# Three paces of one encoder step: transposed decode weights, held stores and one left operand

## The chip, the cores and the metric

The kernel runs on one core of one Trainium2 chip. The metric is the device time of one execution in microseconds (us). Engines: TensorE (PE; its weight loads are PEld), VectorE (DVE), ScalarE (ACT), GpSimd (POOL) and SyncE (SP). Each takes the instructions of its own queue in the order in which the program left them there; transfers are issued from such a queue too.

## The reference, cut to what matters

One layer of a streaming encoder with two kinds of heads, 8 each of width 128. The prompt is one stream of 1024 frames of width 2048; the samples are 8 running streams of 16 frames, with 1024 cached frames each.

```python
h = rms_norm(x, norm_pre)
q_sb, k_sb, v_sb, gate_sb, q_r, k_r, v_r, gate_r = split(h @ w_in)   # q_r, k_r with rope
# stick-breaking attention, strictly causal
z = q_sb @ k_sb.T * HEAD_DIM ** -0.5
log_keep = where(strict, log_sigmoid(-z), 0)
later = cumsum(log_keep, reverse=True) - log_keep
o_sb = where(strict, exp(log_sigmoid(z) + later), 0) @ v_sb
# retention, chunks of 64, state carried on
o_r = (q_r @ k_r.T * intra) @ v_r + (q_r @ s) * decay_read
s = s * gamma ** n + (k_r * decay_write).T @ v_r
# merge
y = concat(head_norm(o_sb) * g_sb * silu(gate_sb), head_norm(o_r) * g_r * silu(gate_r))
x = x + rms_norm(y @ w_out, norm_post)
```

For the samples the same with k_all = concat(cache, k) and v_all = concat(cache, v). Besides x, the new keys, values and states are returned.

## The kernel before, in words

**Products.** Each product of float32 matrices is made of three matmuls of rounded halves: high by high, high by low, low by high. A split is two instructions: ScalarE copies the source into the high half (L174), VectorE subtracts that from the source into the low half (L175). Weights land in `wr` or `wrn` and become `wh` and `wl`, or `whn` and `wln`. Left operands of the last stage land in `mr` and become `mh` and `ml`. Such three matmuls are called a turn.

**Stages.** The tokens are in two groups: group 0 has prompt tiles 0 to 3 and the samples, group 1 prompt tiles 4 to 7. Group 0's heads run from about 30 to 1040 us of the span, group 1's from 1040 to 1860, and then the output projection to the end. In a head the projections run on TensorE all the time (L416 and L473), and attention and retention are laid between them. The output projection is seven products of half-size blocks in the manner of Strassen (numbers 5, 1, 3, 2, 6, 7, 4), each for group 0 and group 1, on lines 1306, 1309 and 1310.

**Paces.** Work beside the projections is written as Python generators. Each time a turn has been recorded, one step of the jobs is recorded too, and `yield n` means "go on n turns later". The numbers of turns are the table at the head of the file. From what was recorded a scheduler then builds each engine's queue; stores and loads with `pin` keep their place in their queue. So a pace shifts where an instruction is recorded, and the queues show where it ends.

**Decode, L862 on.** For each head the 128 rows of the samples against 1024 cached and 128 new keys: scores, sigmoids, a scan on VectorE. The weights go through DRAM to be turned (out on L698, in on L709), VectorE transposes blocks of 32 in place (L942, `kp`), then comes `yield D_TD`, one matmul with the new values (L945, `pd`), and two sets of sixteen with the cached values (L953), each after its own wait `D_VC`, then the evacuation on L961 and L963.

**Out.finish, L769 on.** The outputs of a head are normalised and gated (L771), turned through DRAM in the same manner (`s_o`, L698 and L709), transposed on VectorE (L782), multiplied by the gain (L783), and stored to `s_y` from ScalarE's queue (L786), for group 1 with waits `D_HELD` and pinned. `so` is the tile for stick-breaking, `ro` the one for retention.

**The last stage's operands.** `both(n, groups)`, L1463, makes the jobs that load and split the left operands of product n: `left` loads pairs of `mr` on SyncE (L344, three buffers deep), waits `D_LEFT // 2` = 12 turns, and then splits them one after another. The weights `wr` of the projection are loaded on SyncE (L1323, five buffers). The table `then` starts product 2's operand for group 0 beside product 1 of group 0, whose `left(0, 2)` is read from `s_y`.

Of the kernel before, what the change touches and what calls it, by code (L numbers as in the profile page):

```python
# [47 lines left out]
D_HELD = 7  # L48
# [7 lines left out]
V_SET = 4  # L56
D_SUM = 6
EARLY = 6
D_TD = 7
D_OFF = 3  # L60
N_READ = 40
D_FIN = 2
# [2 lines left out]
D_LEFT = 24  # L65
D_SUM2 = (4, 6, 26)
D_SUM3 = (3, 3, 6)
MR = 3
# [26 lines left out]
def tile_hybrid_step(  # L95
# [48 lines left out]
    wp = ctx.enter_context(tc.tile_pool(name="wp", bufs=4))  # L144
# [27 lines left out]
    def split(hi, lo, src):  # L172
        return (
            nc.scalar.activation(hi, src, AF.Copy),  # L174
            nc.vector.tensor_tensor(lo, src, hi.bitcast(F32), ALU.subtract),  # L175
        )

    def split_pre(hi, lo, src, k):
        return (
            nc.scalar.activation(hi, src, AF.Copy, scale=pre[:, k : k + 1]),  # L180
            nc.vector.scalar_tensor_tensor(  # L181
                lo, src, pre[:, k : k + 1], hi.bitcast(F32), ALU.mult, ALU.subtract
            ),
        )
# [14 lines left out]
    def pin(*made):  # L199
        if anchor[0] is not None:  # L200
            for ins in made:
                tc.add_manual_dep(
                    ins.ins,
                    anchor[0].ins.name,
                    mybir.DependencyInfo(mybir.DependencyClass.NoSync, mybir.DependencyReason.SCHED_ONLY),
                    reason="not ahead of the products",
                )
# [126 lines left out]
    def left(gi, n, hi, lo, bufs, tag, deep, wait, spare=None):  # L334
        src = LEFT[n]
        raw = []

        def load(pair, r=None):
            r = bufs.tile([P, 2, 256], F32, name=tag, tag=tag, bufs=deep) if r is None else r
            if src[0] == "y":  # L340
                rows = s_y[gi][src[1] * H // 2 + pair][:, :, src[2] * 256 : src[2] * 256 + 256]
            else:
                rows = s_s[gi][pair][:, :, src[1], :]
            pin(nc.sync.dma_start(r, rows))  # L344
            raw.extend((r[:, 0], r[:, 1]))

        for pair in range(deep):
            load(pair)
        yield wait
        ahead = deep  # L350
        if spare is not None:
            load(deep, spare.pop().rearrange("p t j d -> p (t j d)")[:, :512].rearrange("p (i n) -> p i n", i=2))
            ahead += 1
            yield 0
        for h in range(HT):
            pin(*split(hi[h], lo[h], raw.pop(0)))
            if h % 2 and h // 2 + deep >= ahead and h // 2 + deep < HT // 2:
                load(h // 2 + deep)
            yield D_OP
# [127 lines left out]
    with ExitStack() as s1:  # L487
# [46 lines left out]
        with tc.tile_pool(name="p0", bufs=2) as p0, tc.tile_pool(name="p0s", bufs=1) as p0s, tc.tile_pool(  # L534
# [97 lines left out]
            for piece, (o, m) in enumerate(X_PIECES[:2]):  # L632
                for w in range(KT // WQ):
# [3 lines left out]
                    for j in range(WQ):  # L637
                        k = w * WQ + j
                        hi, lo = (half[w][:, j, o : o + m] for half in mov)
                        made = split_pre(hi, lo, xc[:, j, :], k)  # L640
# [117 lines left out]
        class Out:  # L758
# [9 lines left out]
            def finish(self, b, gi, h, at, oT, dst):  # L768
                rs = inv_rms(op, self.ssq, P, "o")  # L769
                for i in range(self.nt):  # L770
                    nc.vector.scalar_tensor_tensor(  # L771
                        self.o[:, i, :], self.o[:, i, :], rs[:, i : i + 1], gated[gi, h][:, at + i, b, :], ALU.mult, ALU.mult
                    )
                if gi == 1:
                    yield D_HELD
                s = turn_out(self.o, f"s_o{b}_{h}_{self.nt}_{gi}", held=gi == 1)
                yield D_TO[phase[0]] - (D_HELD if gi == 1 else 0)
                flat = self.o.rearrange("p k d -> p (k d)")
                turn_in(s, flat, back[phase[0]])
                yield D_TI[phase[0]]  # L780
                n = self.nt * P
                tied(nc.vector.transpose(oT[:, :n], flat))  # L782
                nc.vector.tensor_scalar(flat, oT[:, :n], gains[:, b, h : h + 1], None, ALU.mult)  # L783
                if gi == 1:
                    yield D_HELD
                store = nc.scalar.dma_start(dst, flat)  # L786
                if gi == 1:
                    pin(store)
# [76 lines left out]
        def decode(h, qs, rest):  # L865
# [76 lines left out]
            tied(nc.vector.transpose(kp[:, :n], be))  # L942
            yield D_TD
            po = psd.tile([P, 512], F32, name="pd", tag="pd")
# [198 lines left out]
        summed, sampled, lefts, mine = [], [], [], {}  # L1143
        held_over, spare = [], []

        def kept(i):
            return [[half[i][:, h // 2, h % 2 * 256 : h % 2 * 256 + 256] for h in range(HT)] for half in mov]
# [18 lines left out]
        for gi, g in enumerate(GROUPS):  # L1166
            tiles, n, nt = g["tiles"], g["n"], len(g["tiles"])
# [161 lines left out]
        made = collections.deque()  # L1329
# [64 lines left out]
    with ExitStack() as s3:  # L1394
        c3 = s3.enter_context(tc.tile_pool(name="c3", bufs=1))
        rp = s3.enter_context(tc.tile_pool(name="rp", bufs=1))
# [66 lines left out]
        def both(n, groups):  # L1463
            made = []
            for g in groups:
                mine[g, n] = operand(c3, ("ah", "al"), 256, bufs=2) if g else kept(at[n])
                made.append(left(g, n, *mine[g, n], *((rp, "yr", 2) if g else (wp, "mr", MR)), D_LEFT // 2))
            return made

        def jobs_of(made):  # L1470
# [34 lines left out]
        more = Job(sums(fp, [sum_rows(1, h) for h in range(EARLY, H)], D_SUM3, 3), 30)  # L1505
# [202 lines left out]
```

## Time and profile before

| what | us |
|---|---|
| median of three runs (2231.7, 2233.36, 2233.37) | 2233.36 |
| the profiled execution's own time | 2233.32 |
| its span | 2231.6 |
| TensorE busy in the span | 2216.6 (99%) |
| VectorE, ScalarE, GpSimd busy | 1263.4, 920.8, 424.5 |
| 34775 instructions, 12046 of them matmuls | |

The span goes from the first to the last instruction; 1.7 us of the time lie around it. A matmul of 512 columns is listed with 0.39 us, and the next starts 0.23 us after it, since matmuls overlap. In the views a row of waits gives total us, number and longest; a row of the timeline gives start, duration, engine, line, what is written and read, and in brackets the idle time before it with what ended it.

### The profile page before, as it was taken

The numbers are of one execution on the slowest core, as the hardware profiler recorded it, in microseconds if no ns is written. First come the engines' busy times: TensorE is split into PE (matmuls) and PEld (weight loads), VectorE is DVE, ScalarE is ACT, GpSimd is POOL, SyncE is SP. The second block draws the span as 40 slices with busy tenths as digits, with TensorE's granted clock in tenths as the row PEclk, the third lists the DMA queues.
The fourth block names the chain that finished last, engine by engine and source line by source line (L and its number), as shares of the span: only waits on it lengthen the run. The fifth ranks groups of instructions, "written<-read, shape, count | busy, mean of one in ns | idle before, by whom it ended". The sixth has DMA issues, their size and how long they took to land. (4 is left out here: it accounts for less than half of the span.)

```text
span 2231.6 us, 34775 instructions
## 1 busy us (share of the span) xinstructions
PE 2216.6 (99%) x12046; PEld 1887.5 (85%) x12046; DVE 1263.4 (57%) x2690; ACT 920.8 (41%) x1999; POOL 424.5 (19%) x715
## 2 busy tenths in 40 slices
PE   9999999999999999999999999999999999999998
PEld 8888889798888979888788888888888888878887
DVE  5435445453544545346566666757665757656677
ACT  6424333333333333334444343443434445545563
POOL 1022131222213122221222111120202212000020
PEclk9999999999999999999999999999999999999999
DMA  8567565576656557668768787878778777865785
GB/s 295 174 199 199 178 185 181 177 193 217 178 184 184 182 176 195 217 179 289 226 197 230 229 231 221 237 229 237 229 228 223 222 233 197 241 215 166 219 224 170
DMA packets 387234, 467.83 MB, mean 210 GB/s; under 512 B 126321, under 2 KB 243825, under 8 KB 386545
## 3 DMA queue, kind: packets, MB, share of 16 engines
q1 hardware_dynamic: 258928, 291.63, 44.2%
q0 software_dynamic: 36048, 94.67, 15.6%
q10 hardware_dynamic: 92080, 79.32, 11.3%
q8 instruction: 94, 1.54, 0.3%
q14 instruction: 84, 0.68, 0.1%
HBM read 364.56 MB, written 106.95 MB: 211 GB/s over the span
## 5 line engine op out<-in xcount | busy, mean ns | idle before, releaser
L473 PE MATMUL accm<-whn,ml 128*128 128x512 f32 x1152 | 452.3, 393 | 0.0
L473 PE MATMUL accm<-whn,mh 128*128 128x512 f32 x1152 | 451.6, 393 | 0.5 <-DVE rq L519 0.5
L473 PE MATMUL accm<-wln,mh 128*128 128x512 f32 x1152 | 451.9, 392 | 0.0
L174 ACT ACTIVATE wh<-wr 128x512 fp32r<-128x512 f32 x408 | 256.7, 631 | 466.2 <-PE acc L416 191.2
L416 PE MATMUL acc<-ml,wh 128*128 128x256 f32 (+2 forms) x1536 | 446.3, 341 | 0.7 <-DVE ml L181 0.3
L416 PE MATMUL acc<-mh,wl 128*128 128x256 f32 (+2 forms) x1536 | 443.9, 340 | 0.0
L416 PE MATMUL acc<-mh,wh 128*128 128x256 f32 (+2 forms) x1536 | 441.4, 338 | 0.2
L175 DVE TENSOR_TENSOR wl<-wr,wh 128x512 fp32r<-128x512 f32 x408 | 279.4, 688 | 264.6 <-ACT wh L174 244.7
L175 DVE TENSOR_TENSOR wln<-wrn,whn 128x512 fp32r<-128x512 f32 x256 | 175.5, 688 | 285.2 <-ACT whn L174 281.5
L174 ACT ACTIVATE whn<-wrn 128x512 fp32r<-128x512 f32 x256 | 161.2, 631 | 384.4 <-PE accm L473 261.4
L416 PEld LDWEIGHTS acc<-mh,wl 128*128 128x128 f32 x1536 | 281.3, 188 | 23.8 <-issue 5.4
L416 PEld LDWEIGHTS acc<-mh,wh 128*128 128x128 f32 x1536 | 283.0, 188 | 21.0 <-ACT mh L180 0.9
L416 PEld LDWEIGHTS acc<-ml,wh 128*128 128x128 f32 x1536 | 280.3, 188 | 21.1 <-DVE ml L181 1.6
L473 PEld LDWEIGHTS accm<-whn,mh 128*128 128x128 f32 x1152 | 216.5, 188 | 44.6 <-DVE rq L519 0.9
L473 PEld LDWEIGHTS accm<-whn,ml 128*128 128x128 f32 x1152 | 216.5, 188 | 43.2 <-issue 0.8
L473 PEld LDWEIGHTS accm<-wln,mh 128*128 128x128 f32 x1152 | 216.5, 188 | 43.2 <-DVE wln L175 0.3
L745 DVE TENSOR_TENSOR_SCAN kp<-kp 128x1152 f32<-128x1152 f32 (+4 forms) x40 | 82.6, 2064 | 55.9 <-POOL kp L734 28.1
L709 POOL DMA_DIRECT2D be<-s_be x120 | 87.8, 738 | 128.2 <-DMA s_be<-be 128.2
L1306 PE MATMUL a<-wh,mh 128*128 128x512 f32 x240 | 94.7, 395 | 0.1
L1309 PE MATMUL a<-wl,mh 128*128 128x512 f32 x240 | 93.8, 391 | 0.3 <-DVE wl L175 0.2
L1310 PE MATMUL a<-wh,ml 128*128 128x512 f32 x240 | 93.6, 390 | 0.0
L734 POOL TENSOR_SCALAR_AFFINE_SELECT kp<-kp 128x128 f32<-128x128 f32 x40 | 13.8, 345 | 369.2 <-ACT kp L728 369.2
(289 smaller groups left out, 3013.2 us busy)
## 6 DMA issues: line engine op xcount, KB each, us to landing
wrn<-w_rows SPq DMA_DIRECT2D x256, 256.0 KB, 3.9
wr<-w_cols SPq DMA_DIRECT2D x255, 256.0 KB, 4.4
kcT<-cache_k POOLq DMA_DIRECT2D x64, 512.0 KB, 4.7
vc<-cache_v SPq DMA_DIRECT2D x64, 512.0 KB, 5.3
wr<-s_b SPq DMA_DIRECT2D x80, 256.0 KB, 3.4
wr<-w_out SPq DMA_DIRECT2D x80, 256.0 KB, 4.3
br<-w_out SPq DMA_DIRECT2D x64, 256.0 KB, 4.6
s_b<-br ACTq DMA_DIRECT2D x32, 512.0 KB, 4.5
```

Of the source, the lines that this page charges most:

```text
L174: nc.scalar.activation(hi, src, AF.Copy),
L175: nc.vector.tensor_tensor(lo, src, hi.bitcast(F32), ALU.subtract),
L416: last = nc.tensor.matmul(a[:, :m], lhs[:, j, :], rhs[w][:, j, o : o + m], start=(w == 0 and j == 0 and n == 0), stop=(w == KT // WQ - 1 a ...
L473: anchor[0] = nc.tensor.matmul(banks[t], lhs[q][:, j, ts], rhs, start=(k == 0 and n == 0), stop=(k == KT - 1 and n == 2),)
L709: (last if last and i == 3 else q).dma_start(raw[32 * i : 32 * i + 32, :].rearrange("p (k a) -> p k a", a=32), s[:, :, 32 * i : 32 * i + 3 ...
L734: nc.gpsimd.affine_select(blk, blk, pattern=[[-1, P]], base=0, channel_multiplier=1, compare_op=ALU.is_gt, fill=fill,)
L745: nc.vector.tensor_tensor_scan(rev, rev, rev, 1.0, ALU.mult, ALU.bypass)
L1306: ins = nc.tensor.matmul(a, hi[k][:, ts], wh, start=first, stop=False)
L1309: nc.tensor.matmul(a, hi[k][:, ts], wl, start=False, stop=False)
L1310: anchor[0] = nc.tensor.matmul(a, lo[k][:, ts], wh, start=False, stop=last)
```

## The change

Three numbers. `D_TD`, the wait between the transpose of the decode weights and the first matmul that reads them, goes from 7 turns to 9. In `Out.finish` the wait before group 1's store goes from 7 turns to 14. In `both` the wait before the splits of the left operand of product 2 for group 0 goes from 12 turns to 16. A line is added in `both`, so lines from 1465 on have one more.

```diff
-D_TD = 7
+D_TD = 9
...
                 nc.vector.tensor_scalar(flat, oT[:, :n], gains[:, b, h : h + 1], None, ALU.mult)
                 if gi == 1:
-                    yield D_HELD
+                    yield 2 * D_HELD
                 store = nc.scalar.dma_start(dst, flat)
...
                 mine[g, n] = operand(c3, ("ah", "al"), 256, bufs=2) if g else kept(at[n])
-                made.append(left(g, n, *mine[g, n], *((rp, "yr", 2) if g else (wp, "mr", MR)), D_LEFT // 2))
+                more = 4 if (g, n) == (0, 2) else 0
+                made.append(left(g, n, *mine[g, n], *((rp, "yr", 2) if g else (wp, "mr", MR)), D_LEFT // 2 + more))
```

No instruction is added or taken away. In group 0 the queues of SyncE, ScalarE and GpSimd stay as they are. On TensorE, in decode head 0, the first set and L945 keep their place, and the second set of L953 moves. Its rows before, with the turns around it (`acc` is the projection's sum, `pd` the decode output, the numbers name buffers):

```order
L416 MATMUL acc0_2125<-ml3_158,wh_2275 128x256
L416 MATMUL acc1_2126<-ml3_158,wh_2275 128x384
L953 MATMUL pd_2144<-vc_1999,kp_1197 32x256 x4
L953 MATMUL pd_2144<-vc_2053,kp_1197 32x256 x4
L953 MATMUL pd_2144<-vc_2181,kp_1197 32x256 x4
L953 MATMUL pd_2144<-vc_2183,kp_1197 32x256 x4
L416 MATMUL acc0_2125<-mh3_157,wl_2276 128x256
L416 MATMUL acc1_2126<-mh3_157,wl_2276 128x384
L416 MATMUL acc0_2336<-mh0_151,wh_2340 128x256
L416 MATMUL acc1_2337<-mh0_151,wh_2340 128x384
```

and now:

```order
L416 MATMUL acc0_2125<-mh3_157,wl_2276 128x256
L416 MATMUL acc1_2126<-mh3_157,wl_2276 128x384
L416 MATMUL acc0_2320<-mh0_151,wh_2324 128x256
L416 MATMUL acc1_2321<-mh0_151,wh_2324 128x384
L416 MATMUL acc0_2320<-ml0_152,wh_2324 128x256
L416 MATMUL acc1_2321<-ml0_152,wh_2324 128x384
L953 MATMUL pd_2148<-vc_1999,kp_1197 32x256 x4
L953 MATMUL pd_2148<-vc_2053,kp_1197 32x256 x4
L953 MATMUL pd_2148<-vc_2201,kp_1197 32x256 x4
L953 MATMUL pd_2148<-vc_2203,kp_1197 32x256 x4
L416 MATMUL acc0_2320<-mh0_151,wl_2325 128x256
```

The set moved behind six matmuls of the projection; heads 1 to 5 show the same, and head 6 a move by two matmuls.

In group 1 neighbours change places at many points. One is the end of head 6, at about 1750 us. On VectorE, before (`be` and `so` on L782 and L783 are the turned outputs, L745 and L746 the attention scan of the next rows):

```order
L745 SCALAR_TENSOR_TENSOR kp_17388<-kp_17388 128x640
L782 STREAM_TRANSPOSE be_16850<-so_16433 128x512
L746 TENSOR_TENSOR be_17389<-be_17389,kp_17388 128x640
L783 TENSOR_SCALAR so_16433<-be_16850,pre_77 128x512
L175 TENSOR_TENSOR wln_17510<-wrn_17507,whn_17509 128x512
L175 TENSOR_TENSOR wln_17559<-wrn_17556,whn_17558 128x512
L175 TENSOR_TENSOR wln_17595<-wrn_17592,whn_17594 128x512
```

and now:

```order
L782 STREAM_TRANSPOSE be_16853<-so_16434 128x512
L783 TENSOR_SCALAR so_16434<-be_16853,pre_77 128x512
L745 SCALAR_TENSOR_TENSOR kp_17389<-kp_17389 128x640
L746 TENSOR_TENSOR be_17390<-be_17390,kp_17389 128x640
L175 TENSOR_TENSOR wln_17513<-wrn_17510,whn_17512 128x512
L175 TENSOR_TENSOR wln_17548<-wrn_17545,whn_17547 128x512
L175 TENSOR_TENSOR wln_17595<-wrn_17592,whn_17594 128x512
```

L782 and L783 moved ahead of the scan, and further down L1108 ahead of L521. On ScalarE at the same place, before (`s_b` on L329 is another store, `sw` on L517 and L518 the rope's swapped halves):

```order
L329 DMA s_b1_7_120<-br_17256 512x1x256
L174 ACTIVATE whn_17509<-wrn_17507 128x512
L174 ACTIVATE whn_17558<-wrn_17556 128x512
L786 DMA s_y1_2_139<-so_16433 128x512
L174 ACTIVATE whn_17594<-wrn_17592 128x512
L517 ACTIVATE sw_17450<-acc0_17349 64x512
L518 ACTIVATE sw_17450<-acc0_17349 64x512
```

and now:

```order
L329 DMA s_b1_7_120<-br_17250 512x1x256
L786 DMA s_y1_2_139<-so_16434 128x512
L174 ACTIVATE whn_17512<-wrn_17510 128x512
L174 ACTIVATE whn_17547<-wrn_17545 128x512
L174 ACTIVATE whn_17594<-wrn_17592 128x512
L517 ACTIVATE sw_17450<-acc0_17349 64x512
L518 ACTIVATE sw_17450<-acc0_17349 64x512
```

The store of L786 moved ahead of two splits. The third place is the last stage at about 1966 us, the splits of the left operand of product 2. ScalarE before:

```order
L174 ACTIVATE wh3_19611<-wr3_19609 128x512
L174 ACTIVATE wh3_19627<-wr3_19625 128x512
L174 ACTIVATE mh0_10327<-mr_19568 128x256
L174 ACTIVATE wh3_19645<-wr3_19643 128x512
L174 ACTIVATE mh0_10327<-mr_19568 128x256
L174 ACTIVATE wh3_19660<-wr3_19658 128x512
L174 ACTIVATE mh0_10327<-mr_19570 128x256
```

and now:

```order
L174 ACTIVATE wh3_19611<-wr3_19609 128x512
L174 ACTIVATE wh3_19626<-wr3_19624 128x512
L174 ACTIVATE wh3_19641<-wr3_19639 128x512
L174 ACTIVATE mh0_10327<-mr_19568 128x256
L174 ACTIVATE wh3_19658<-wr3_19656 128x512
L174 ACTIVATE mh0_10327<-mr_19568 128x256
L174 ACTIVATE wh3_19673<-wr3_19671 128x512
```

VectorE before (`br` on L326 are sums of weight blocks made beside it):

```order
L175 TENSOR_TENSOR wl3_19612<-wr3_19609,wh3_19611 128x512
L326 TENSOR_TENSOR br_19511<-br_19511 128x256
L175 TENSOR_TENSOR ml0_10328<-mr_19568,mh0_10327 128x256
L175 TENSOR_TENSOR wl3_19628<-wr3_19625,wh3_19627 128x512
L326 TENSOR_TENSOR br_19511<-br_19511 128x256
L175 TENSOR_TENSOR ml0_10328<-mr_19568,mh0_10327 128x256
L175 TENSOR_TENSOR wl3_19646<-wr3_19643,wh3_19645 128x512
L326 TENSOR_TENSOR br_19511<-br_19511 128x256
L175 TENSOR_TENSOR wl3_19661<-wr3_19658,wh3_19660 128x512
```

and now:

```order
L326 TENSOR_TENSOR br_19511<-br_19511 128x256
L175 TENSOR_TENSOR wl3_19627<-wr3_19624,wh3_19626 128x512
L326 TENSOR_TENSOR br_19511<-br_19511 128x256
L175 TENSOR_TENSOR wl3_19642<-wr3_19639,wh3_19641 128x512
L175 TENSOR_TENSOR ml0_10328<-mr_19568,mh0_10327 128x256
L326 TENSOR_TENSOR br_19511<-br_19511 128x256
L175 TENSOR_TENSOR ml0_10328<-mr_19568,mh0_10327 128x256
L175 TENSOR_TENSOR wl3_19659<-wr3_19656,wh3_19658 128x512
L175 TENSOR_TENSOR wl3_19674<-wr3_19671,wh3_19673 128x512
```

Two `wl` moved ahead of the first `ml`. On ScalarE one `wh` moved ahead of the first `mh` and one more ahead of the second: the fourth `wh` of the rows, wh3_19660 before and wh3_19658 now, stood behind the second `mh` and stands ahead of it, while on VectorE its `wl` stands behind the second `ml` in both. On SyncE the fourth load of `mr` moved from ahead of the fifth of five `wr` loads to behind it.

## The prediction

> **What bounds the kernel now.** I read the busy times first, then stretches of the span one by one, then the waits of TensorE (PE), then the timeline where those waits are.
>
> ```profile
> PE 2216.6 (99%) x12046; PEld 1887.5 (85%) x12046; DVE 1263.4 (57%) x2690; ACT 920.8 (41%) x1999; POOL 424.5 (19%) x715
> ```
>
> TensorE's matmuls fill 2216.6 of the 2231.6 us of the span; no other engine passes 57%, apart from the weight loads that run beside the matmuls. The change adds no instruction and removes none, so it can only act on the 15.0 us in which TensorE stands. The next view says where those are. Its columns are the stretch, its length, then PE, PEld, DVE, ACT and POOL busy.
>
> ```profile
> 0.00:30.00 30.00, 27.95 (x168) 25.47 (x169) 20.97 (x43) 21.11 (x43) 0.69 (x6) 1.00 0.86 297
> 30.00:1040.00 1010.00, 1008.46 (x6221) 879.46 (x6220) 469.39 (x1076) 365.12 (x785) 235.76 (x421) 1.00 0.65 194
> 1040.00:1860.00 820.00, 819.48 (x4018) 684.42 (x4017) 530.01 (x1064) 342.21 (x735) 154.39 (x244) 1.00 0.80 228
> 1860.00:1990.00 130.00, 128.35 (x597) 104.89 (x596) 86.19 (x178) 73.17 (x164) 13.80 (x21) 1.00 0.81 233
> 2200.00:2231.60 31.60, 22.42 (x122) 19.37 (x120) 23.17 (x66) 8.81 (x29) 2.55 (x3) 0.89 0.68 200
> ```
>
> The head loses 2.05 us and the tail 9.18, and no edit is there. Group 0 (30 to 1040) loses 1.54, group 1 (1040 to 1860) 0.52, the start of the final stage 1.65; the stretch left out, 1990 to 2200, loses nothing. The waits of TensorE show what ends nearly all of that:
>
> ```profile
> PE pd L945 <- DVE kp L942: 1.5, 7, 0.5
> PE pb L565 <- DVE ones L538: 1.2, 1, 1.2
> PE a L1309 <- DVE wl L175: 1.0, 3, 0.7
> PE accm L473 <- DVE rq L519: 0.5, 1, 0.5
> PE pa L999 <- DVE so L851: 0.4, 1, 0.4
> PE acc L416 <- DVE ml L181: 0.3, 1, 0.3
> ```
>
> Each row is total us, number, longest. The three edits touch the first, the fourth and one of the three waits in the third row. These are 1.5 + 0.5 + 0.7 = 2.7 us, and I take 0.2% of the time, 4.5 us, as about what a measurement of this kernel can tell from no change. Matmuls overlap, so a gap understates what it costs: one below shows 0.66 and costs 0.82 by the starts on either side of it, 0.16 more. With that on nine waits the most that can be gained is 2.7 + 1.4 = 4.1 us.
>
> **Part one, the wait after the transpose (7 to 9 turns).** The place is the same in each of the first seven decode heads; this is head 0:
>
> ```profile
> 210.94 1.37 DVE L942 STREAM_TRANSPOSE kp<-be 128x1152 f32<-128x1152 f32 x1
> 211.53 0.46 PE L416 MATMUL acc<-mh,wh 128*128 128x256 f32 x2
> 212.46 0.46 PE L945 MATMUL pd<-vv,kp 128*128 128x128 f32 x2 [0.47 <-DVE kp L942]
> ```
>
> VectorE (DVE) ends the transpose at 212.31 and TensorE, done with line 416 at 211.99, starts L945 at 212.46. For two more turns of three matmuls to help, either L942 would have to stand earlier in VectorE's queue or L945 later in TensorE's. The order shows neither: both keep their rows in heads 0 to 6, as does the first set of sixteen L953. Only the second set goes one turn, six matmuls here, back; it has long had its transposed weights, so that costs nothing. What covers the second set's evacuation, which goes behind three rope operations, is that nothing on TensorE waits for it; if that cover were gone it would be one wait of some 0.5 us like the one above. I cost part one at 0, between −2.6 (all seven gaps with 0.16 more each) and +0.5.
>
> **Part two, the held store (14 turns for 7).** What it does is again read from the order, not from the yield: of the stores on L786 only a few move, and the one beside a wait goes earlier. The end of head 6 of group 1:
>
> ```profile
> L709 SPq DMA_DIRECT2D so<-s_o x4: 326/484/592, 1742.6 to 1744.2; - x4
> DMA to landing us min/median/max: 2.7/2.9/3.1
> ...
> 1750.28 1.59 DVE L745 TENSOR_TENSOR_SCAN kp<-kp 128x640 f32<-128x640 f32 x1 [3.71 <-POOL kp L734]
> 1751.79 0.68 DVE L782 STREAM_TRANSPOSE be<-so 128x512 f32<-128x512 f32 x1
> 1753.10 0.47 DVE L783 TENSOR_SCALAR so<-be,pre 128x512 f32<-128x512 f32 x1
> 1753.61 0.34 ACTq L786 DMA_DIRECT2D s_y<-so  x1
> 1754.05 0.63 ACT L174 ACTIVATE whn<-wrn 128x512 fp32r<-128x512 f32 x1 [2.60 <-PE acc L416]
> 1754.70 0.60 ACT L517 ACTIVATE sw<-acc 64x512 f32<-64x512 f32 x1
> 1755.31 0.59 ACT L518 ACTIVATE sw<-acc 64x512 f32<-64x512 f32 x1
> 1755.77 0.39 PE L473 MATMUL accm<-wln,mh 128*128 128x512 f32 x1
> 1755.93 0.69 DVE L519 TENSOR_TENSOR rq<-acc,cosT 128x512 f32<-128x512 f32 x1 [0.53 <-ACT sw L518]
> 1756.68 0.50 PE L473 MATMUL accm<-whn,mh 128*128 128x512 f32 x1 [0.52 <-DVE rq L519]
> ```
>
> The first two lines are of the view of L709 alone. ScalarE (ACT) has the store's issue ahead of the third whn, and the store waits for L783, which waits for scan and transpose. So L517, L518, VectorE's L519 and TensorE's panel all stand behind a store that they don't need. In the new order L782 and L783 come before the scan, in VectorE's 3.71 us of idleness, and the store comes ahead of all three whn. Its data landed by 1744.2 + 3.1 = 1747.3; with 0.68 + 0.47 = 1.15 the two are done by 1748.5, 1.8 us before the scan can start. Then whn, L517, L518 and L519 go 0.35 us earlier (1753.70 against 1754.05; the 0.34 of the store is gone), and of the wait 0.17 + 0.16 remain: −0.35. Bounds: nothing, if the accumulators that L517 reads are what comes late, and −0.68, the whole loss. After it, L1108 (0.7 us) stands ahead of L521 on VectorE, and TensorE has the products on that result a turn later; I take these two as even.
>
> With every block moved by a turn, many neighbours in group 1 change places on all four queues, SyncE's included. TensorE loses 0.52 us in those 820, and VectorE works 530 of them, so a swap has room. For new waits I take +0.2, a third of one like the above (0.68); bounds 0 and three of them, +2.0.
>
> **Part three, the left operand (first wait 12 turns to 16).** In the final stage, in product 2's left operand for group 0:
>
> ```profile
> 1962.81 1.14 ACT L174 ACTIVATE wh<-wr 128x512 fp32r<-128x512 f32 x2
> 1966.70 0.42 ACT L174 ACTIVATE mh<-mr 128x256 fp32r<-128x256 f32 x1 [2.76 <-DMA mr<-s_y]
> 1967.15 0.43 DVE L175 TENSOR_TENSOR ml<-mr,mh 128x256 fp32r<-128x256 f32 x1 [0.95 <-ACT mh L174]
> 1967.19 0.39 PE L1306 MATMUL a<-wh,ah 128*128 128x512 f32 x1
> 1967.50 0.68 DVE L175 TENSOR_TENSOR wl<-wr,wh 128x512 fp32r<-128x512 f32 x1
> 1968.24 0.50 PE L1309 MATMUL a<-wl,ah 128*128 128x512 f32 x1 [0.66 <-DVE wl L175]
> 1970.05 0.63 ACT L174 ACTIVATE wh<-wr 128x512 fp32r<-128x512 f32 x1 [2.10 <-DMA wr<-w_out]
> 1970.59 0.40 ACT L174 ACTIVATE mh<-mr 128x256 fp32r<-128x256 f32 x1
> 1970.71 0.69 DVE L175 TENSOR_TENSOR wl<-wr,wh 128x512 fp32r<-128x512 f32 x1 [0.92 <-ACT wh L174]
> 1971.46 0.50 PE L1309 MATMUL a<-wl,ah 128*128 128x512 f32 x1 [0.16 <-DVE wl L175]
> ```
>
> The wl of 1967.50 has its wh since 1963.95; it stands behind an ml that waits for a mh that waits for a transfer. That costs 1968.24 − 1967.19 − 0.23 = 0.82 us. In the new order this wl and the next come ahead of that ml, and this loss goes. The chain of waits says what is late next:
>
> ```profile
> 1964.10 5.84 DMA wr<-w_out
> 1970.05 0.64 ACT wh L174
> ```
>
> That block of weights lands at 1969.94 whatever TensorE does, for the transfers ahead of it on SyncE are the same in both. Its wh can't start before 1970.05, nor its wl before 1970.71. On VectorE two ml stand ahead of this wl, as before; but the second's mh, which came before this wh on ScalarE, now comes behind it. So: wh to 1970.63, mh to 1970.99 (1970.59 + 0.40), ml of 0.43 from about 1971.0, wl of 0.69 from about 1971.4, TensorE at 1972.10 where it now starts at 1971.46. The 0.82 is waited out again here, and 0.64 more. The fourth load of mr, on SyncE, is issued after that ml, at about 1971.4, and its mh stands ahead of a wh: +0.1 for that. Part three: +0.74, between −1.15 (both losses gone: 0.82, and 0.16 + 0.16) and +1.6 (0.64, and the mr load as late as 1 us).
>
> The Trainium skill, in "Perfetto Trace Analysis", section "Optimization Strategy", says to find the gaps on the engine that bounds, see which instruction ends each, and have it start sooner; by that each gap that is named is worth its length, 2.7 us, and the sum would be about 2230.6. The rows of 1964.10 and 1970.05 speak against it here: a gap is paid back where the next thing that the same engine needs comes at a fixed time. The same page, section "Tensor Engine Instruction (MATMUL, LD_WEIGHTS)", says that ScalarE and VectorE take their queues strictly in order; the trace agrees, for the wl of 1967.50 stood 3.5 us with its wh done.
>
> **Sum:** 0 − 0.35 + 0.2 + 0.74 = +0.6 us on the profiled execution's 2233.32, which is the median of the runs shown (2233.36) within 0.04: 2233.9.
>
> **Rivals.** *Part three pays* (14%). If the block of 1969.94 lands two us earlier, as with less traffic in front of it, neither loss comes back: 0 − 0.35 + 0.2 − 1.15 gives 2232.0. For it speaks that loads of wr are issued earlier once two wl are; against it that this one was issued at 1964.10, before the swap.
>
> *Part one does lift the seven waits* (5%), because the transposes run sooner after all, from earlier work on VectorE: −1.5 to −2.6 on the forecast, 2231.3 to 2232.4. Against it stand the unchanged rows of both queues up to 1040 us; they speak for the plain failure of this part to do what it says, which the forecast has in it.
>
> *Each gap pays its length* (2%): nothing late comes behind any of them, so 2.7 to 4.1 us go, 2229.2 to 2230.6. It needs the two above at once. The Trainium skill, "Perfetto Trace Analysis", section "Optimization Strategy", would have this one.
>
> *Slower by more than 0.2%* (4%): L782 now holds up the scan if the turned rows land late. It has 1.8 us to spare; beyond that each us goes to the scan, to the wln behind it and to L519, on which TensorE already waits. To reach +4.5 with the +0.6 it takes 3.9 + 1.8 = 5.7 us, a landing 8.8 us after issue for 3.1. The block of weights above took 5.84, which would cost 5.84 − 3.1 − 1.8 = 0.9 us: 2234.8.
>
> **How the numbers follow.** My forecast, orders changed and little moved, has 75%, the rivals 14, 5, 2 and 4. The ends of the forecast's own terms, −0.7 in part two, up to +2.0 in group 1 and +1.6 in part three, reach 2232.9 to 2236.5; the runs shown scatter from 2231.7 to 2233.37, which opens the low end. With the rival of part three and most of part one's, the range is 2231.0 to 2236.4. Faster than 2228.9 needs nearly all of the 4.1 us that there are, and the head's wait of 1.2 with it: 3%, the rival of all gaps and a little more. Slower than 2237.8: the last rival, 4%. The rest, 93%, is no change that can be told.
>
> **What would show it.** In the profile after: the L945 waits at about 1.5 us in seven places with the first at 212.46; the L473 wait on L519 near 1756 down to 0.2 or gone, with the store before 1750; no wait at 1968, and one of about 1.4 us at 1972 in its place, ended by a wl whose queue was held by ml; line 1309's row at about 1.5 to 2 us in all; the stretch 1040 to 1860 within 0.5 of 819.5 busy. I am wrong if the L945 row falls below 1, if TensorE passes 1972 without waiting, or if a new wait of over 1 us stands in group 1.

## The result, and the profile after

| | runs | median us | lowest to highest |
|---|---|---|---|
| before | 16 | 2232.97 | 2231.53 to 2235.43 |
| after | 16 | 2236.93 | 2234.23 to 2241.30 |

The ratio is 1.0018, with a 95% interval of 1.0011 to 1.0024: 4.0 us slower (2.5 to 5.4). That is under the 4.5 us taken as the bound of "no change", but 0.5 us above the range of 2231.0 to 2236.4. The runs after also spread wider, over 7 us where those before spread over 4.

The profiled execution after took 2235.63 us (span 2233.9), 1.3 under the median of its kernel, so it shows less of the loss than most executions have. The stretches of its span, columns as in the prediction, and the waits of TensorE:

```profile
30.00:1040.00 1010.00, 1007.77 (x6217) 878.72 (x6216) 473.13 (x1078) 364.70 (x785) 235.60 (x421) 1.00 0.64 194
1040.00:1860.00 820.00, 818.54 (x4011) 682.65 (x4010) 529.43 (x1061) 341.02 (x733) 153.44 (x243) 1.00 0.79 228
1860.00:1990.00 130.00, 127.72 (x596) 104.87 (x595) 86.70 (x179) 73.46 (x165) 14.23 (x22) 1.00 0.80 238
```

```profile
PE pd L945 <- DVE kp L942: 1.5, 7, 0.5
PE a L1309 <- DVE wl L175: 1.4, 3, 0.9
PE pa L848 <- DVE kp L811: 1.4, 1, 1.4
PE pb L565 <- DVE ones L538: 1.2, 1, 1.2
PE acc L416 <- ACT mh L180: 0.9, 1, 0.9
PE accm L473 <- DVE rk L519: 0.7, 1, 0.7
```

Group 1 (1040 to 1860) has lost 1.46 us where it lost 0.52, though the L519 wait near 1756, all of that 0.52 before, is no longer in the list. In its place stands a new one, L848 on L811: the matmuls of the attention's last and longest rows in head 3, which wait for VectorE to transpose their turned weights. The seven L945 waits are untouched. (The L519 wait on `rk` is at 42 us, in group 0, which the held store does not reach; it came and went in the runs below in kernels whose queues there are the kernel's before, so it belongs to the execution.)

The chain of waits of that stretch, after, begin and length in us:

```profile
1410.64 6.53 DMA s_be<-be
1417.16 0.02 issue
...
1419.38 6.58 DMA be<-s_be
...
1426.15 1.26 DVE kp L811
1427.41 0.04 issue
1427.45 0.60 PE pa L848 x3
```

The rows go out to DRAM on L698, come back on L709, VectorE transposes them, TensorE starts. Before, the same place had no wait of a matmul, and yet no margin. The rows of its timeline, and its wait list for the weight loads of TensorE:

```profile
1425.12 1.25 DVE L811 STREAM_TRANSPOSE kp<-be 128x1024 f32<-128x1024 f32 x1 [2.31 <-DMA be<-s_be]
1426.42 0.97 PEld L848 LDWEIGHTS pa<-vo,kp 128*128 128x128 f32 x8 [0.22 <-DVE kp L811]
1426.47 1.12 PE L848 MATMUL pa<-vo,kp 128*128 128x128 f32 x8
```

```profile
PEld pa L848 <- DVE kp L811: 0.8, 3, 0.4
```

VectorE waited 2.31 us for that transfer, the weight load 0.22 for VectorE, and the matmul came just as its predecessors ended: whatever lands later costs its whole lateness.

That is the sign of being wrong which the prediction gave last: a new wait of over 1 us in group 1.

### The profile page after: what moved, and what is told of

The parts are those of the page before. It is cut to its first block, busy times and chain, and to the rows that moved or that the text cites. A ratio compares the mean times of both kernels' runs of the same rounds, so it can differ in the third digit from the quotient of the medians.

```text
span 2233.9 us, 34763 instructions
## 1 busy us (share of the span) xinstructions
PE 2215.9 (99%) x12046; PEld 1886.6 (84%) x12046; DVE 1267.3 (57%) x2690; ACT 920.2 (41%) x1999; POOL 424.2 (19%) x715
## 4 chain that ended last, share of the span: by engine, by line
PE 91%; DMA 3%; DVE 2%; issue 1%; ACT 1%; SPq 0%; DVEq 0%; POOL 0%; ACTq 0%; POOLq 0%
PE accm L473 35%; PE acc L416 32%; PE a L1309 4%; PE a L1310 4%; PE a L1306 4%; PE z L821 2%; PE pa L848 2%; PE pd L953 1%; PE zc L892 1%; DMA wr<-w_out 1%; PE rs L980 1%; PE pa L999 1%; PE pS L1016 1%; PE pa L1006 1%; DMA xc<-x_cols 1%
## 5 line engine op out<-in xcount | busy, mean ns | idle before, releaser
L709 POOL DMA_DIRECT2D be<-s_be x120 | 87.8, 738 | 130.9 <-DMA s_be<-be 130.9
L745 DVE TENSOR_TENSOR_SCAN kp<-kp 128x1152 f32<-128x1152 f32 (+4 forms) x40 | 82.5, 2062 | 48.0 <-POOL kp L740 27.9
L1306 PE MATMUL a<-wh,mh 128*128 128x512 f32 x240 | 94.7, 395 | 0.0
L1309 PE MATMUL a<-wl,mh 128*128 128x512 f32 x240 | 93.7, 390 | 0.3 <-DVE wl L175 0.3
```

The lines of the kernel that those rows point to most:

```text
L709: (last if last and i == 3 else q).dma_start(raw[32 * i : 32 * i + 32, :].rearrange("p (k a) -> p k a", a=32), s[:, :, 32 * i : 32 * i + 3 ...
L745: nc.vector.tensor_tensor_scan(rev, rev, rev, 1.0, ALU.mult, ALU.bypass)
L1306: ins = nc.tensor.matmul(a, hi[k][:, ts], wh, start=first, stop=False)
L1309: nc.tensor.matmul(a, hi[k][:, ts], wl, start=False, stop=False)
```

## Experiments

Theory A, after the first comparison: the loss is that round trip, put off by a swap which the held store causes in group 1; the other two paces cost little. Rival B: group 0's moved second set. Rival C: the last stage loses more than the profiled execution shows. All runs below were compared with the kernel before on the same chip; the table has the medians' difference and the ratio's interval. An interval that reaches from under 1 to over 1 doesn't tell the kernel from the one before. The wait read from a run is that of its one profiled execution.

| kernel | us against before | ratio, 95% interval |
|---|---|---|
| decode pace 9 alone | +1.0 | 0.9997 to 1.0015 |
| store held 14 alone | +3.1 | 1.0006 to 1.0024 |
| left operand alone | +1.0 | 0.9998 to 1.0016 |
| all three | +4.3 | 1.0008 to 1.0026 |
| before, split behind | +1.7 | 0.9997 to 1.0015 |
| held 14, split ahead | +1.9 | 0.9998 to 1.0016 |
| held 28 | +1.4 | 0.9999 to 1.0017 |
| held 9 | +5.9 | 1.0017 to 1.0035 |
| held 14, two orders restored | +0.4 | 0.9992 to 1.0010 |
| before, two orders swapped | +1.9 | 0.9996 to 1.0014 |
| all three, two orders restored | +2.9 | 1.0003 to 1.0021 |
| before, one copy more | +1.2 | 0.9997 to 1.0014 |
| pace 9 and operand | +1.8 | 0.9998 to 1.0016 |
| operand, one order restored | +0.4 | 0.9992 to 1.0010 |
| decode pace 24 | −1.9 | 0.9982 to 1.0000 |
| pace 24 and operand with its order | −0.9 | 0.9986 to 1.0004 |

**One part at a time.** The decode pace alone:

```diff
-D_TD = 7
+D_TD = 9
```

> Only the decode pace of 9 turns; the held store and the left operand stay as before. Theory A (the loss is the turned attention rows of group 1, which the held store reshuffles): this part touches none of it, so within 0.5 us of before, and the seven L945 waits stay at 1.5 us in all. Rival B (the loss is run-to-run jitter in group 0 set loose by the second set of sixteen moved back): 1.5 us or more slower. Rival C (all of it is the left operand): within 0.5 us.

The held store alone:

```diff
                 if gi == 1:
-                    yield D_HELD
+                    yield 2 * D_HELD
                 store = nc.scalar.dma_start(dst, flat)
```

> Only the store held 14 turns; the other two paces stay as before. Theory A: 2.5 to 3.5 us slower than before, with a wait of TensorE on L811 of 1 us or more near 1426 us, and the L519 wait at 1756 nearly gone. Rival B and rival C: within 0.7 us of before, since by them group 1 hides its swaps.

The left operand alone:

```diff
-                made.append(left(g, n, ..., D_LEFT // 2))
+                more = 4 if (g, n) == (0, 2) else 0
+                made.append(left(g, n, ..., D_LEFT // 2 + more))
```

> Only the left operand's splits four turns later. Theory A: 0.5 to 0.8 us slower, no wait at 1968 and one of about 1 us near 1971. Rival C (the last stage loses more in most runs than in the one profiled): 2.5 us or more slower. Rival B: within 0.5 us of before.

And all of them again:

> The changed kernel itself again, for a second profile and as the sum of the three above on the same chip: 3 to 5 us slower than before by every theory. Theory A: the wait on L811 near 1426 us is there again, and its length differs from the 1.4 us of the first profile, since transfers set it. If it is not there while the time is as long, theory A falls.

The held store carries most of the loss, as theory A had it. Its profile, and that of all three, have the wait on L811 in the same place, each of another length (1.4 in the first profile):

```profile
PE pa L848 <- DVE kp L811: 2.0, 1, 2.0
```

```profile
PE pa L848 <- DVE kp L811: 2.7, 1, 2.7
```

The profiles of the other two parts have none over 0.1 there. So the held store makes the wait, and its length differs from one profile to the next. The decode pace and the operand stand at +1.0 each, and neither is told apart from nothing; theory A had expected at most 0.5 of the first and 0.5 to 0.8 of the second, and these two times alone exclude neither rival B (1.5 or more) nor rival C (2.5 or more). The traces speak against both. From the first L945 (212.5 us before) to the first L848 at 1189.7 us, all five profiles with the pace of 9 take about 0.1 us less than the kernel before, so the moved second set costs group 0 nothing; and from the first L1306 to the end the profile of the operand alone is 0.7 us longer. In the profile of the pace alone, 0.9 of the 1.2 us that its span is longer lie ahead of that L945.

**What follows the wait.** In these two profiles the wait costs more than its length. The clock granted to TensorE, the third number from the right, is halved for 3.4 us from the first matmul after the wait. First the held store alone, then all three again:

```profile
1420.00:1425.00 5.00, 5.00 (x23) 1.00 1.20 173
1427.40:1430.80 3.40, 3.40 (x16) 0.50 0.84 285
```

```profile
1429.20:1432.60 3.40, 3.40 (x17) 0.51 0.83 266
```

Eight matmuls of L848 take 2.08 us there, where they took 1.12 before:

```profile
1427.40 2.08 PE L848 MATMUL pa<-vo,kp 128*128 128x128 f32 x8 [1.98 <-DVE kp L811]
```

At half the clock, 3.4 us do the work of 1.7, so 1.7 us are lost on top of the wait. Take two landmarks, the rows of L848 on `vo` that begin at 1291.3 and at 1494.4 us before. From one to the other the held store alone takes 3.8 us longer than before: 2.1 of lost starts at L848 and 1.7 of the clock. The change's second profile takes 4.5 longer, 2.8 and 1.7; its first, which kept the full clock, 1.5 longer, all of it lost starts. What brings the clock down is open: waits of 2.0 (held 28) and 2.4 us (one copy more) left it at 1.00. Over whole executions, a granted clock under 0.998 is on record for 9 of the 48 of the change and of the store held 14 and 9 turns alone, and for none of the 143 of the other kernels tried. Three of the nine are among the sixteen in the first table, at 2238.44, 2240.91 and 2241.30 us, three of the four slowest: this is a part of the wider spread.

**One split moved.** What the held store swaps at head 3, about 30 us ahead of the wait, is a `wh` split on ScalarE. Before, it stands ahead of four pairs of evacuations (L507, L508); with the store held it stands behind them. A ScalarE row of before and one of a kernel in which nothing but this swap was made:

```profile
1395.84 0.61 ACT L174 ACTIVATE wh<-wr 128x512 fp32r<-128x512 f32 x1
```

```profile
1401.74 0.68 ACT L174 ACTIVATE wh<-wr 128x512 fp32r<-128x512 f32 x1
```

The split frees a buffer of `wr`, and the next load into it is at the head of SyncE's queue. SyncE's rows, before and with the swap:

```profile
1397.20 0.33 SPq L405 DMA_DIRECT2D wr<-w_cols  x1
1400.24 1.20 SPq L299 DMA_DIRECT2D br<-w_out  x2
1403.89 1.27 SPq L405 DMA_DIRECT2D wr<-w_cols  x2
```

```profile
1403.17 0.33 SPq L405 DMA_DIRECT2D wr<-w_cols  x1
1403.59 1.20 SPq L299 DMA_DIRECT2D br<-w_out  x2
1404.90 2.02 SPq L405 DMA_DIRECT2D wr<-w_cols  x3
```

One buffer free 6 us later holds two loads of `br` behind it, and seven loads then go within 5 us, just ahead of the turned rows. The edit adds one order to the kernel before (an edge for the scheduler alone, no wait; the edits from here on are shortened):

```diff
-            split(wh, wl, wr)
+            made = split(wh, wl, wr)
+            # third split behind head 3's panel in group 1 only
+            tc.add_manual_dep(made[0].ins, gates[1][1].ins.name, NoSync, SCHED_ONLY)
```

> The kernel before, with one order added: in group 1, head 3, the third split of the weights that follow the gate panel stands behind the panel's four evacuations on ScalarE (L507, L508) and not ahead of them. No pace is changed. Theory A (that split is what delays the turned attention rows: its block of wr comes free some 5 us later, SyncE's queue stands behind it, and its loads then go together with the turned rows): 1 to 2.7 us slower, with a wait of TensorE on L811 of 1 us or more near 1426 us. Rival D (many small swaps in group 1 add up): 0.3 us slower at most and no such wait.

And the other way round, in the kernel with the store held:

```diff
+            tc.add_manual_dep(gates[0][0].ins, made[0].ins.name, NoSync, SCHED_ONLY)
```

> The store held 14 turns, as in the run of that part alone, and one order added: that same split stands ahead of the evacuations, where the kernel before has it. All other swaps of the held store stay. Theory A: the wait on L811 near 1426 us is gone (under 0.3 us) and the time is within 0.7 us of before. Rival D: 2.5 to 3 us slower, as without the order.

In the kernel before, the swap alone makes a wait of 0.6 us, less than the 1 us or more that theory A expected; the median, +1.7, is within its 1 to 2.7, with an interval that holds zero. Restored in the held kernel it takes the wait from 2.0 to 0.8 and the median loss from 3.1 to 1.9, two times whose intervals overlap. Theory A expected under 0.3 and under 0.7, so the split is one cause and not the only one.

**The store's wait by itself.** Rival E says that what costs is the later arrival of the stored rows.

```diff
-                    yield D_HELD
+                    yield 28
```

> Only the store's wait, 28 turns for 7, twice what the change has. Its order has that split ahead of the evacuations, as before. Theory A: no wait of more than 0.5 us on L811 near 1426 us, and within 1.2 us of before. Rival E (what costs is that the rows reach their readers later): slower than the 14 turns, 3 us or more.

```diff
-                    yield D_HELD
+                    yield 9
```

> Only the store's wait, 9 turns for 7. Its order has that split behind the evacuations. Theory A: the wait on L811 near 1426 us is there with 1 us or more, and the time is 1.5 to 3 us above before, though the store is held only two turns longer. Rival E: 0.5 us at most, two sevenths of what the 14 turns cost.

Rival E fell with the 9 turns: two turns more cost 5.9 us (3.8 at least by the interval) where it allowed 0.5. With 28 turns the median is lower than with 14, though the intervals overlap. Where the orders end decides, not how long the store is held. Theory A was right on 9 turns at this place (1.7 us there), but not on the time: of the 5.2 us by which that profile's span is longer, 2.3 lie in the last stage. It was wrong on 28 turns, whose profile has 2.0 us there with the split ahead. The two legs of the round trip say more.

**Two legs.** The legs are read from each trace: the issue of the store on L698 to its landing, and that landing to the last landing of the reads on L709. The last column is how much longer than before the stretch between the two landmarks is.

| kernel | out | back | wait | stretch |
|---|---|---|---|---|
| before | 5.1 | 8.9 | 0.0 | 0.0 |
| left operand alone | 5.1 | 8.8 | 0.0 | −0.1 |
| decode pace 9 alone | 5.4 | 8.9 | 0.1 | +0.2 |
| pace 24 and operand with its order | 5.6 | 9.2 | 0.7 | +0.9 |
| before, split behind | 6.0 | 8.9 | 0.6 | +0.8 |
| before, one copy more | 7.6 | 8.9 | 2.4 | +2.6 |
| before, two orders swapped | 6.2 | 9.7 | 1.6 | +1.8 |
| held 14, split ahead | 5.1 | 9.6 | 0.8 | +1.0 |
| held 14, two orders restored | 5.5 | 9.3 | 1.0 | +1.2 |
| all three, two orders restored | 5.7 | 9.1 | 1.0 | +1.2 |
| held 14 | 5.8 | 10.1 | 2.0 | +3.8 |
| held 28 | 6.1 | 9.8 | 2.0 | +2.4 |
| held 9 | 5.9 | 9.8 | 1.7 | +1.9 |
| the change, first profile | 6.5 | 8.8 | 1.4 | +1.5 |
| the change, second profile | 7.1 | 9.5 | 2.7 | +4.5 |

In each row with a wait of 0.6 us or more, the wait is the sum of the legs less a constant: about 14.2 us with the store at its old pace, about 13.9 with the store held, where TensorE is ready for L848 some 0.3 us sooner after the issue. And the stretch is longer by the wait and 0.2 us of overlap, but for held 28 (0.2 more) and the two with the halved clock: this wait is what costs there.

The first four rows have the orders of the kernel before at this place, and so have the pair, the operand with its order and pace 24. Over these seven profiles the way out is 5.0 to 5.6 us, the way back 8.7 to 9.2, and one of them waits 0.7 us: so small is the margin that part of the wait comes and goes with the execution.

Beyond that scatter the way out is long where loads go just ahead of it. The view of the transfers between issue and landing of that store, before and after; the row of digits has the busy share of the transfer engines after, in tenths, for 40 slices of 0.165 us:

```profile
DMA packets 829, 1.43 MB, mean 280 GB/s; under 512 B 48, under 2 KB 485, under 8 KB 828
```

```profile
DMA  9999999999999999999897987898532100000018
DMA packets 1155, 1.81 MB, mean 274 GB/s; under 512 B 83, under 2 KB 687, under 8 KB 1154
```

0.38 MB more pass in the 1.4 us more. That alone is no proof of a cause, since what is moved during a longer leg is more in any case, and the rate isn't the same everywhere. Here are the same view of the split behind (6.0 us) and of held 28 (6.1 us):

```profile
DMA packets 1233, 1.96 MB, mean 327 GB/s; under 512 B 93, under 2 KB 686, under 8 KB 1232
```

```profile
DMA packets 336, 0.87 MB, mean 143 GB/s; under 512 B 43, under 2 KB 49, under 8 KB 335
```

In the change the transfer engines are busy for 70% or more of the first 4.6 us of the leg, and then for half or less until it ends; in held 28 little passes beside the store, which takes 6.1 us all the same. So a part of the way out isn't a shared path, and what makes that part is open.

The way back has its own swap: on SyncE a quarter of the turned rows (L709) moved ahead of one `wr` load. It waits for the store to land, so the load behind it goes out in the midst of the reads. The next edits restore both orders, or swap both.

```diff
+        # on top of the split's order: head 3's quarter behind the 13th load of wr
+        tc.add_manual_dep(quarters[2].ins, blocks[start[0] + 12].ins.name, NoSync, SCHED_ONLY)
```

> The store held 14 turns alone, and two orders added in group 1, head 3, both as the kernel before has them: the split ahead of the evacuations on ScalarE, and on SyncE one load of wr ahead of the quarter of the turned rows that is read back there (that quarter waits for the store of the rows, and whatever stands behind it goes out in the midst of the reads). All other swaps of the held store stay. Theory F (the wait on L811 is set by the round trip of the turned rows, 5.1 us out and 8.9 us back before, and each of the two swaps puts weight loads into one of the two legs): no wait over 0.3 us on L811 near 1426, legs of 5.1 to 5.4 and 8.8 to 9.1 us, and the time within 1 us of before. Rival D (the many other swaps cost it): still 1.9 us slower or more, as with the split alone restored.

```diff
-        tc.add_manual_dep(quarters[2].ins, blocks[start[0] + 12].ins.name, NoSync, SCHED_ONLY)
+        tc.add_manual_dep(blocks[start[0] + 12].ins, quarters[2].ins.name, NoSync, SCHED_ONLY)
```

> The kernel before with the same two orders the other way round, as the held store has them, and nothing else. Theory F: a wait on L811 of 1.3 to 2.5 us near 1426, both legs longer than before (5.8 or more, 9.5 or more), and 1.5 to 3 us slower. Rival D: no more than the 1.7 us of the split alone, with a wait of 0.6 us.

The same two restored orders in the changed kernel:

```diff
-D_TD = 7
+D_TD = 9
...
-                    yield D_HELD
+                    yield 2 * D_HELD
...
+                more = 4 if (g, n) == (0, 2) else 0
...
+            tc.add_manual_dep(gates[0][0].ins, made[0].ins.name, NoSync, SCHED_ONLY)
+        tc.add_manual_dep(quarters[2].ins, blocks[start[0] + 12].ins.name, NoSync, SCHED_ONLY)
```

> The changed kernel with all three paces and the two orders restored as in the run of the held store. Theory F: the wait on L811 near 1426 is gone, and 1 to 2 us are left above before, which are the decode pace's and the left operand's. Rival D: 3.5 us or more, as the change itself.

And a transfer that no order explains, from memory to memory, in the kernel before, every queue else the same:

```diff
+                    (gi, h) == (1, 3) and pin(nc.sync.dma_start(s_copy, w_out[0, :P, :1024]))
                     acc = acc or project(g, mov, col(4, h))
```

> The kernel before with one transfer of 0.5 MB more, from memory to memory, on SyncE behind the head's weight loads at about 1407 us, so that it is under way when the turned rows go out at 1411; every queue is else as before. Theory F: the outward leg takes 0.7 us or more longer than 5.1, TensorE waits 0.3 to 1.5 us on L811 near 1426, and the kernel is 0.5 to 1.5 us slower. Rival G (the queues' order makes TensorE wait by itself, not the sharing of the transfers): no wait there, within 0.3 us of before.

The last one shows that other transfers lengthen the way out: in its profile 0.5 MB more takes it from 5.1 to 7.6 us and makes TensorE wait 2.4 us, more than expected (0.3 to 1.5), in a kernel whose orders are else those of before. Its median, +1.2, is not told from zero. The two swaps bring both legs up and 1.6 us of wait, inside theory F's range.

Restoring the two orders brings the time from +3.1 to +0.4 by medians, but both profiles with them restored, that of the held store and that of the change, still have 1.0 us there, where theory F expected at most 0.3 in the first and none in the second. Their legs (5.5 and 9.3, 5.7 and 9.1) are at the upper end of the scatter above, and 0.3 us of the wait is TensorE's being ready sooner. In the change itself, restoring them left 2.9 of 4.3 us, more than the 1 to 2 expected; its interval overlaps that of the change, so the time does not show the gain. That profile, the slowest of its executions, lost most in the last stage (waits on L1306 and L1309 of 3.7 us in all).

**The other two paces.**

```diff
-D_TD = 7
+D_TD = 9
...
+                more = 4 if (g, n) == (0, 2) else 0
```

> The decode pace of 9 and the left operand four turns later, without the held store. If each of the two costs about 1 us, as their medians alone have it, the pair is 1.5 to 2.5 us slower; if the operand alone costs (0.7 by its order) and the pace nothing, 0.4 to 1.1 us; if both medians were chance, within 0.4 us. In no case a wait on L811 near 1426 over 0.3 us.

The pair stands where the two single medians put it, at +1.8, its interval still holds zero, and no wait on L811 is in its profile. For the operand, one order more on ScalarE:

```diff
+            # the wh whose weights land last, behind the second mh of product 2
+            tc.add_manual_dep(seen[5].ins, pair2[2].ins.name, NoSync, SCHED_ONLY)
```

> The left operand's splits four turns later, alone, and one order added on ScalarE: its second mh stands ahead of the wh whose weights land last, as in the kernel before. If the loss in the last stage is that mh, behind that wh, holding up the wl on VectorE, the wait on L1309 near 1970 falls from about 1.1 us of lost starts to 0.5 or less, and the time to 0.5 us above before or under it. If the loss is the landing of the weights, the wait stays at about 1 us.

The wait there fell from 1.14 us of lost starts with the operand alone to 0.50 (0.87 and 0.23 by the rows), and the median from +1.0 to +0.4, within the intervals. Then the pace that does move L945:

```diff
-D_TD = 7
+D_TD = 24
```

> Only the decode pace, 24 turns for 7. In its order the first matmul after the transpose (L945) stands six projection turns later on TensorE in heads 0 to 6, which it does not with 9. If a gap is worth its length there, the seven waits on L942 are gone and the kernel is 1.5 to 2.6 us faster; if what is put off is waited for elsewhere, the waits are gone and the time is within 0.5 us of before or above it.

All seven waits are gone, and the kernel is 1.9 us faster by medians; its interval ends at 1.0000. In its profile the transpose of head 0 now ends 1.1 us before the weight load of L945:

```profile
210.69 1.37 DVE L942 STREAM_TRANSPOSE kp<-be 128x1152 f32<-128x1152 f32 x1
213.16 0.37 PEld L945 LDWEIGHTS pd<-vv,kp 128*128 128x128 f32 x2
213.34 0.38 PE L945 MATMUL pd<-vv,kp 128*128 128x128 f32 x2
```

```diff
-D_TD = 7
+D_TD = 24
...
+                more = 4 if (g, n) == (0, 2) else 0
...
+            tc.add_manual_dep(seen[5].ins, pair2[2].ins.name, NoSync, SCHED_ONLY)
```

> The decode pace of 24 and the left operand four turns later with the one order restored; no held store. If the two act in their own stages, the sum of what each did alone: 1.9 us faster for the pace and nothing for the operand, so 1.5 to 2 us faster, with the seven L945 waits gone, no wait near 1968 and one of about 0.5 us of lost starts near 1970. If the last stage takes back what came before it, within 0.5 us of before.

−0.9 us, under the sum expected, with an interval that holds zero. A part of the difference shows in its profile: a wait of 0.7 us on L811 at 1426, with the store at its old pace. The operand's shift adds nothing that can be seen. In the profile of the pace of 24 alone, the slowest of its executions, TensorE is 2.3 us ahead of before at the first L1306 and has lost it again at the end. Of the kernels here the pace of 24 alone has the lowest median, 2231.27 against 2233.16.

## Why the prediction missed, step by step

**The step that failed** is the term for new waits in group 1: "+0.2, a third of one like the above", bounds 0 to +2.0, argued from "VectorE works 530 of them, so a swap has room". It measured 1.4 to 2.7 us of wait at one place in the three profiles with the store held 14 turns and no order restored, 1.7 us more in two of them where the clock fell after it, and +3.1 in the median for that part. The room on VectorE was beside the point: what ran out was the margin of a transfer, two queues away. I had looked for margins in the wait list of the matmuls, where L848 did not stand; the weight loads' list had it, three times, 0.8 us. The last rival came nearest: it had turned rows land late, but of the outputs (L709 into `so`) and not of the attention weights, at 1750 and not at 1410.

**Part one: right.** The seven waits stayed at 1.5 us, as the unchanged rows said. The measured +1.0 is not told apart from the 0 forecast. That the gap is worth its length when it really goes was tested by the pace of 24: −1.9 of the −1.5 to −2.6 given as that rival's price. The Trainium skill, "Perfetto Trace Analysis", section "Optimization Strategy", says to make what is waited for start sooner or complete faster; here the transpose came when it came before (210.69 us, 210.94 before) and its reader went later, which closed the gaps as well.

**Part two's gain: right at its place.** The third row below is the panel's start behind L519; its matmul row no longer shows a wait over 0.02.

```profile
1748.71 0.71 DVE L782 STREAM_TRANSPOSE be<-so 128x512 f32<-128x512 f32 x1 [0.54 <-DMA so<-s_o]
1751.58 0.48 ACTq L786 DMA_DIRECT2D s_y<-so  x1
1758.22 0.19 PEld L473 LDWEIGHTS accm<-whn,mh 128*128 128x128 f32 x1 [0.44 <-DVE rq L519]
```

L782 goes ahead of the scan and the store ahead of the splits. 0.18 us of lost starts remain of 0.68, a gain of 0.5 for the 0.35 forecast. L782 itself waited 0.54 us for its rows, but behind L783 VectorE stood idle for 2.38 us more before the scan, so the swap had room on VectorE and the last rival's price wasn't paid here.

**Part three: right in mechanism at its place.** No wait at 1968, one later, ended by a wl behind an ml behind a mh behind the wh whose weights land last. These are the rows after:

```profile
1970.64 0.63 ACT L174 ACTIVATE wh<-wr 128x512 fp32r<-128x512 f32 x1 [1.98 <-DMA wr<-w_out]
1971.18 0.40 ACT L174 ACTIVATE mh<-mr 128x256 fp32r<-128x256 f32 x1
1971.61 0.42 DVE L175 TENSOR_TENSOR ml<-mr,mh 128x256 fp32r<-128x256 f32 x1 [2.15 <-ACT mh L174]
1971.95 1.29 DVE L175 TENSOR_TENSOR wl<-wr,wh 128x512 fp32r<-128x512 f32 x2
1972.69 0.50 PE L1309 MATMUL a<-wl,ah 128*128 128x512 f32 x1 [0.87 <-DVE wl L175]
```

The wait cost 1.08 us of lost starts for the 1.46 forecast, and restoring the mh took half of it away, as that mechanism demands. The part's time, +1.0, agrees with the +0.74, without being told from zero. From the first L1306 to the end, the 0.7 us of the operand alone stand beside 0.5 and 0.0 in the change's two profiles. Kernels without the operand's shift differ there from before by −0.7 to +0.6 us, and two of them, held 9 and the decode pace of 24, by 2.3 and 2.4. So the profiles don't tell this part from chance either.

**The range** ended lower than the prediction's own bounds allow: +0.5, 0, +2.0 and +1.6 on 2233.32 make 2237.4, and not 2236.4, and the median of 2236.93 lies under that. A hit there would have been luck: the bound of +2.0 for new waits came from waits of 0.68 us, not from a transfer's margin, and the held store alone passed it by its median. The one profile taken first, at 2235.63, also lies within the range and under most executions of its kernel.

**Open:** which of the last stage's waits belong to a kernel and which to an execution; why held 28 has a long way out with the split ahead and little moved beside it; what brings the clock down after one wait and not after another.

## What to carry to other kernels

Before saying that a swap is hidden, look for readers with no margin: a weight load that waits although its matmul does not is one, and so is a transpose that waits for a transfer just ahead of its reader. Price such a wait at more than its length where the granted clock can fall after it: here 1.7 us came on top in two profiles. Follow each such chain back through its transfers, and ask of every swap which load now stands behind which wait in the queue that issues loads. A pace in a scheduled program need not move the instruction that it names: 9 turns left L945 in its place and 24 moved it. Read the order at several values before pricing one.

## What the runs showed that I had not expected

A store of 0.5 MB took 5.1 us with 1.43 MB moved in that time, itself included, and 7.6 us with one copy of 0.5 MB more under way and 2.14 MB moved:

```profile
DMA packets 1524, 2.14 MB, mean 281 GB/s; under 512 B 93, under 2 KB 1065, under 8 KB 1523
```

How much is moved doesn't tell its time, though: 0.87 MB went with 6.1 us, 1.96 MB with 6.0. A wait of TensorE of 2.0 us, and one of 2.7, was followed by 3.4 us at half the granted clock, and one of 2.4 was not. And one split of 0.6 us on ScalarE, moved behind 5 us of evacuations, reached TensorE 25 us later by way of a buffer, SyncE's queue and the transfers.
